# Out-projections of a two-layer diffusion backbone: residual and modulation steps by turns, z fetched in halves, read-back on GpSimd's queue, and a gMLP u phase in program order

## Chip, core and metric

The kernel runs on one core of one Trainium2 chip. The metric is the device time of one execution in microseconds (us). The engines are TensorE (PE in the profile; PEld is its weight load), VectorE (DVE), ScalarE (ACT), GpSimd (POOL) and SyncE (SP), which only issues transfers here.

## What is computed

512 latent tokens and 256 context tokens of width 1024 go through two layers. Each layer is FFN, mixer, FFN; the mixer is a gated MLP (gMLP) in layer 0 and grouped-query attention in layer 1. Every sub-layer is modulated by a shift, a scale and a gate, and closed by a LayerNorm. Everything is float32.

```python
def ffn_sublayer(x, shift, scale, gate, w_in, w_out, ln_g, ln_b):
    y = swiglu(x * (1 + scale) + shift, w_in, w_out)        # D_FF = 2816
    return layer_norm(ALPHA * x + 0.5 * gate * y, ln_g, ln_b)

def gmlp_mix(h, w_in, sgu_g, sgu_b, w_s, b_s, w_out):        # half width 3072
    u, v = split(gelu(h @ w_in), 2)
    v = layer_norm(v, sgu_g, sgu_b)
    v = einsum('gpq,bnqgc->bnpgc', w_s, v.reshape(...)) + b_s   # 8 groups, chunks of 128 tokens
    return (u * v) @ w_out

def modulation(cond, w_mod, b_mod):                          # 9 vectors of 1024 per layer
    return split(silu(cond) @ w_mod + b_mod, 9)              # for c and for c_ctx
```

The last sub-layers work on the latent tokens alone.

## The kernel before

**Numbers.** Each float32 operand is split into a high part and a remainder ("low"): ScalarE writes the high part, VectorE subtracts it. A product is three matmuls: high x high, high x low, low x high. The tokens lie in 6 blocks of 128 (4 latent, 2 context).

**Weights.** `load_raw` lets SyncE fetch raw weight tiles (256 KB, 6 buffers); `pump` turns them into split units `w` (8 buffers). `split_later` puts the low subtraction on a list, and `flush` issues the list.

**Order.** TensorE, SyncE and GpSimd's transfers issued through `self.pool` keep program order (`Pinned`). VectorE and ScalarE keep it only between `pin(True)` and `pin(False)`; elsewhere a scheduler may move their instructions. The u phase of gMLP runs unpinned.

**Fills.** The modulation vectors of later sub-layers are made in the background. `begin_sublayer` queues the units of `MOD_PLAN`; a unit is one of the nine vectors, for one or two conditions (`nconds`). Each call of `fill` does one of a unit's 16 steps: it takes a 256 KB tile of w_mod from `mraw`, does one VectorE step per condition into `acc`, and asks for the next tile. After eight steps GpSimd adds over the partitions (`partition_all_reduce`, L370) and sends the row away (L371). In an FFN's input projection `tile_strassen` calls it once per tile through `slot`, from f = 2 on. `End.begin` does what is left of the queue at one go.

**Activations.** The input projection makes 22 (FFN) or 24 (gMLP) tiles of 128 x 768. The last 4 stay in SBUF; the others are stored to DRAM by GpSimd (`act<-stage`). `Acts.feed` reads them back into `q` buffers (6 of them, two per tile, up to three tiles in hand) on SyncE's queue, and `prepare` splits a tile three tiles ahead of its use.

**Out-projection** (`out_proj`, for three FFNs and gMLP). Two halves of 512 columns; per half a loop over the tiles x: 18 matmuls each, a `pump`, a `prepare`, then VectorE work at the end of the tile. At x = 1 of half 0 the residual begins: all six blocks of z (512 KB each) and two rows of ln_g and ln_b are asked for on SyncE's queue, and from x = 3 on each tile multiplies and adds one half block (`residual`). Half 0 of z goes first, then a second pair of rows and half 1. Each of these tiles calls `fill` as well. In half 1 the result of half 0 is added to z in tiles 1 to 6 (`adds`). The last 6 tiles of half 1 are done block by block with the LayerNorm (`End`). The first FFN has no residual step (`prev` is None): z is the input. `out_proj_latent` is the same for the last FFN, with both halves at once.

**u phase of gMLP.** v was stored to DRAM before (`v_spill`). Each of 24 passes j does the spatial matmuls of v tile j, the projection of u tile j + 1, then on VectorE the six S steps that empty the spatial banks; v tile j + 1 is normalized (`normed`: ScalarE, then a split), the Gelu of u tile j is taken and multiplied by S. v tile j + 2 is fetched in pass j (`fetch`, three buffers); so a v tile is asked for one pass before it is normalized.

Of the kernel before, what the change touches and what calls it, by code (L numbers as in the profile page):

```python
# [63 lines left out]
    [(1, 5), (1, 2), (1, 3)],  # L64
    [(1, 6), (1, 4), (1, 7)],
    [],
# [19 lines left out]
class Backbone:  # L86
# [68 lines left out]
    def slot(self, post, n=1, fills=0):  # L155

        self.flush()
        self.pump(n)
        if self.combining is not None:
            post()  # L160
            if next(self.combining, self) is self:
                self.combining = None
        else:
            self.fill(fills)
            post()
# [182 lines left out]
    def mod_unit(self, l, i):  # L348

        nc, io = self.nc, self.io  # L350
        nconds = self.nconds(l, i)
        m = self.mods[l, i] = self.dram.tile([2, D], F32, name=f"mod{l}{i}")
        for c in range(nconds):
            self.pool.dma_start(m[c : c + 1, :], io["b_mod"][l, i * D : i * D + D].unsqueeze(0))
        for half in range(2):
            accs = [self.acc() for _ in range(nconds)]
            for k in range(KD):
                raw, dve = self.next_raw(), self.dve
                for c in range(nconds):
                    cs = self.cs[:, c * KD + k : c * KD + k + 1]  # L360
                    if k:
                        dve.scalar_tensor_tensor(accs[c], raw, cs, accs[c], ALU.mult, ALU.add)
                    else:
                        dve.tensor_scalar(accs[c], raw, cs, None, ALU.mult)
                self.filler_raw()
                if k < KD - 1:
                    yield
            s = slice(half * 512, half * 512 + 512)
            for c in range(nconds):
                nc.gpsimd.partition_all_reduce(accs[c], accs[c], P, bass_isa.ReduceOp.add)  # L370
                nc.gpsimd.dma_start(m[c : c + 1, s], accs[c][0:1, :], accum_op=ALU.add)  # L371
            yield
        self.mod_sent.add((l, i))
        if i % 3 == 2:
            self.mod_done.add((l, i))
        elif {(l, i - i % 3), (l, i - i % 3 + 1)} <= self.mod_sent:
            self.later(READ_LATER, lambda: self.mod_columns(l, i - i % 3))
# [22 lines left out]
    def residual(self, prev, nblocks):  # L400

        for b in range(nblocks):
            self.sp.dma_start(self.z[b], self.zsrc[b])
        if prev is None:
            return
        for half in range(2):
            s = slice(half * 512, half * 512 + 512)
            rows = []
            for name in ("ln_g", "ln_b"):
                row = self.zplace()  # L410
                src = self.io[name][prev[0], prev[1], s].unsqueeze(0)
                self.sp.dma_start(row, src.to_broadcast([P, 512]))
                rows.append(row)
            for _ in range(1 if half else 3):
                yield
            for b in range(nblocks):
                z = self.z[b][:, s]
                self.dve.tensor_tensor(z, z, rows[0], ALU.mult)
                self.dve.tensor_tensor(z, z, rows[1], ALU.add)
                yield  # L420

# [48 lines left out]
    def fill(self, n=1):  # L470

        for _ in range(n):
            with self.behind():
                for x in self.pending:
                    x[0] -= 1
                due = [x for x in self.pending if x[0] < 0]
                self.pending = [x for x in self.pending if x[0] >= 0]
                for _, f in due:
                    f()
                next(self.filler, None)  # L480

    @contextmanager
# [230 lines left out]
    def out_proj(self, acts, l, i, factor, end, prev, gate_at=2):  # L713
# [5 lines left out]
        self.new_z(NB)  # L719
        residual = iter(())  # L720
        st = self.stats(NB)
        banks, adds = {}, []
        for half, order in enumerate(orders):
            body = n - CLOSE * half
            for x in range(body):
# [15 lines left out]
                if not half and x == 1:  # L741
                    residual = self.residual(prev, NB)
                    next(residual, None)
                if not half and x == gate_at:
                    self.load_gate(l, i + 2, NB)
                if adds and x:
                    b, z, tmp = adds.pop(0)
                    self.dve.tensor_tensor(z, z, tmp, ALU.add)
                    self.dve.bn_stats(st[b][:, 0], z)
                else:  # L750
                    next(residual, None)
                if not half or x > 3:
                    acts.feed(half, 3 - half)
                if half or x < n - 2:
                    self.fill(1)
        for _ in residual:
            pass
        rest = [acts.of(f) for f in orders[1][n - CLOSE :]]
# [14 lines left out]
    def out_proj_latent(self, acts, l, i, factor, end, prev):  # L773
# [4 lines left out]
        self.new_z(NB_LAT)  # L778
        residual = iter(())
        banks = {}  # L780
        for x in range(n - CLOSE_LAT):
            ws = self.weights(2)
            for b in range(NB_LAT):
# [4 lines left out]
                if b % 2:  # L788
                    self.flush()
                    self.pump(1)  # L790
                    if b == 1:
                        acts.prepare(0, x + AHEAD + 1)
                        next(residual, None)
            self.release(2)
            acts.feed(0, 4)
            if x == 1:
                residual = self.residual(prev, NB_LAT)
                next(residual, None)
                self.load_gate(l, i + 2, NB_LAT)
        for _ in residual:  # L800
            pass
        st = self.stats(NB_LAT)
# [134 lines left out]
    def ffn(self, l, i, nblocks, end, prev):  # L937
# [4 lines left out]
        for f in range(FF):  # L942
            opened = self.begun.pop(min(self.begun)) if self.begun else None
            self.tile_strassen(lambda: acts.place(f), opened, int(f > 1))
            if not f:
# [120 lines left out]
    def gmlp(self, l, i, nblocks, end, prev):  # L1066
# [74 lines left out]

        fetch(0)
        fetch(1)
        var = self.const.tile([P, NB], F32, name="v_var")
# [29 lines left out]

        vns = [normed(3)]
        for j in range(GMLP_CH):
# [15 lines left out]
            banks = us.pop(0)  # L1192
            fetch(j + 2)
            m, done = acts.place(j)
# [6 lines left out]
            for step in range(2):  # L1201
                for bb in range(NB // 2):
# [4 lines left out]
                    )  # L1207
            if j + 1 < GMLP_CH:
                vns.append(normed(NB if j else 3))
            for x, ps in enumerate(banks):  # L1210
# [3 lines left out]
                dve.tensor_tensor(to, u[:, cols], S[:, cols], ALU.mult)  # L1214
                done(cols, to)
                self.flush()
            with nullcontext() if j else self.tc.issue_after(self.last_split):
                self.pump()
            self.fill(int(0 < j < GMLP_CH - 1))
# [435 lines left out]
    def body(self):  # L1655
# [4 lines left out]
        self.last_rstd = self.last_low = None  # L1660
        self.lows, self.slots, self.filler = [], False, iter(())
        self.setup()
# [19 lines left out]
class Acts:  # L1682
# [40 lines left out]
    def feed(self, half, most):  # L1723

        wanted = self.wanted[half]
        while len(self.raw) < most and wanted:
            f = wanted.pop(0)
            parts = []
            for o in range(0, self.ntok, self.width):
                raw = self.k.q(512)[:, 0 : self.width]  # L1730
                cols = slice(o, o + self.width)
                self.k.sp.dma_start(raw, self.dram[f][:, cols])
                parts.append((cols, raw))
# [160 lines left out]
```

## Time and profile before

| what | us |
|---|---|
| median of 3 runs (lowest, highest) | 2899.09 (2896.8, 2903.82) |
| profiled execution | 2898.31 |
| its span, first to last instruction | 2896.5 |
| busy: PE | 2795.1 |
| busy: DVE | 2108.4 |
| busy: ACT | 1163.6 |
| busy: POOL | 411.2 |

The profile is of one execution. A row of the timeline gives the start and the duration in us, the engine, the line of the kernel, the operation, what it writes <- what it reads, the shapes, how many instructions are merged, and in brackets how long the engine stood idle before and what ended that. Many operations go through a helper and carry its line, L81. SPq marks SyncE's issue of a transfer. A row of the stretches gives start:end and length, then for each engine its busy time and the number of instructions, the granted clock of TensorE, the busy share of the DMA engines and GB/s.

### The profile page before, as it was taken

The numbers are of one execution on the slowest core, as the hardware profiler recorded it, in microseconds if no ns is written. First come the engines' busy times: TensorE is split into PE (matmuls) and PEld (weight loads), VectorE is DVE, ScalarE is ACT, GpSimd is POOL, SyncE is SP. The second block draws the span as 40 slices with busy tenths as digits, with TensorE's granted clock in tenths as the row PEclk, the third lists the DMA queues.
The fourth block names the chain that finished last, engine by engine and source line by source line (L and its number), as shares of the span: only waits on it lengthen the run. The fifth ranks groups of instructions, "written<-read, shape, count | busy, mean of one in ns | idle before, by whom it ended". The sixth has DMA issues, their size and how long they took to land.

```text
span 2896.5 us, 40499 instructions
## 1 busy us (share of the span) xinstructions
PE 2795.1 (96%) x14454; PEld 2507.2 (87%) x14454; DVE 2108.4 (73%) x3692; ACT 1163.6 (40%) x2232; POOL 411.2 (14%) x379
## 2 busy tenths in 40 slices
PE   7899999999999999999999999999999989999998
PEld 5899988888899977889999788999978778888887
DVE  7988877577776787498787968877785578733445
ACT  6333432532344432453333226333432556633322
POOL 1010112234301112000010210000021121100001
PEclk9999999999999999999999999999999999999999
DMA  7433375355544474344335644433474423454352
GB/s 240 132 112 124 106 248 169 135 186 179 184 156 142 145 245 141 117 148 126 121 118 195 197 127 132 143 119 119 134 250 149 130 84 52 139 147 135 102 168 97
DMA packets 407090, 426.84 MB, mean 147 GB/s; under 512 B 27944, under 2 KB 308584, under 8 KB 406888
## 3 DMA queue, kind: packets, MB, share of 16 engines
q1 hardware_dynamic: 387400, 361.36, 40.3%
q0 software_dynamic: 19488, 62.90, 6.8%
q8 instruction: 113, 1.85, 0.3%
q14 instruction: 89, 0.73, 0.1%
HBM read 362.95 MB, written 63.41 MB: 147 GB/s over the span
## 4 chain that ended last, share of the span: by engine, by line
PE 72%; DVE 9%; DMA 8%; ACT 6%; issue 3%; SPq 1%; POOL 0%; DVEq 0%; ACTq 0%; POOLq 0%
PE ps L81 71%; DMA v<-v_spill 3%; ACT v L1135 2%; DVE w L81 2%; DVE acc L81 1%; DMA zraw<-in_ln_b_dram 1%; DVE w L148 1%; PE pp L81 1%; DMA q<-act 1%; SPq L81 1%; DVE z L81 1%; ACT w L147 1%; DMA mraw<-in_w_mod_dram 1%; ACT q L566 1%; DMA raw<-in_w_mod_dram 1%
## 5 line engine op out<-in xcount | busy, mean ns | idle before, releaser
L81 PE MATMUL ps<-comb,w 128*128 128x384 f32 x5544 | 974.1, 336 | 21.5 <-DVE comb L81 12.5
L81 PEld LDWEIGHTS ps<-comb,w 128*128 128x128 f32 x5544 | 963.9, 188 | 27.9 <-DVE comb L81 15.8
L81 PE MATMUL ps<-w,acts 128*128 128x512 f32 x3768 | 867.6, 391 | 19.6 <-DVE acts L81 19.3
L81 PEld LDWEIGHTS ps<-w,acts 128*128 128x128 f32 x3768 | 704.6, 188 | 174.7 <-DVE acts L81 29.1
L81 ACT CAST w<-raw 128x512 fp32r<-128x512 f32 x583 | 360.5, 619 | 732.3 <-PE ps L81 675.0
L81 DVE TENSOR_TENSOR w<-raw,w 128x512 fp32r<-128x512 f32 x583 | 426.8, 737 | 249.6 <-ACT w L81 249.5
L81 PE MATMUL ps<-h,w 128*128 128x384 f32 (+2 forms) x2304 | 447.9, 354 | 7.0 <-DVE su L1205 3.5
L81 PEld LDWEIGHTS ps<-h,w 128*128 128x128 f32 x2304 | 404.9, 189 | 45.1 <-DVE w L148 3.9
L370 POOL PARTITION_ALL_REDUCE acc<-acc x56 | 200.5, 3587 | 787.2 <-DVE acc L81 693.8
L81 PE MATMUL ps<-w,h 128*128 128x512 f32 x1200 | 278.5, 393 | 5.9 <-DVE kT L142 3.1
L81 PEld LDWEIGHTS ps<-w,h 128*128 128x128 f32 x1200 | 226.5, 190 | 54.9 <-ACT h L580 3.6
L81 DVE TENSOR_TENSOR q<-q,ps 128x384 f32<-128x384 f32 (+1 forms) x282 | 157.2, 558 | 151.0 <-PE ps L81 125.1
L81 DVE SCALAR_TENSOR_TENSOR acc<-mraw,cs,acc 128x512 f32<-128x512 f32 x340 | 248.3, 764 | 3.8 <-DMA mraw<-in_w_mod_dram 3.8
L81 ACT CAST w<-sums 128x512 fp32r<-128x512 f32 x198 | 122.9, 621 | 235.9 <-DVE sums L290 113.7
L81 ACT CAST acts<-q 128x384 fp32r<-128x384 f32 (+1 forms) x262 | 129.5, 521 | 199.4 <-DMA q<-act 160.2
L81 POOL DMA_DIRECT2D act<-stage x84 | 47.4, 565 | 995.3 <-DVE stage L81 803.2
L148 DVE TENSOR_TENSOR w<-raw,w 128x512 fp32r<-128x512 f32 x161 | 112.1, 714 | 77.3 <-ACT w L147 76.8
L81 DVE TENSOR_TENSOR acts<-q,acts 128x384 fp32r<-128x384 f32 (+1 forms) x262 | 138.5, 562 | 9.6 <-ACT acts L81 9.6
L81 DVE TENSOR_TENSOR w<-sums,w 128x512 fp32r<-128x512 f32 x198 | 135.6, 685 | 1.9 <-ACT w L81 1.9
L147 ACT CAST w<-raw 128x512 fp32r<-128x512 f32 x161 | 96.3, 619 | 57.1 <-PE ps L81 32.0
L174 POOL TENSOR_TENSOR rs<-ve,mhalf 128x1 f32<-128x1 f32 (+3 forms) x47 | 40.7, 867 | 491.5 <-DVE ve L171 260.9
L81 DVE TENSOR_TENSOR z<-z,zraw 128x512 f32<-128x512 f32 x88 | 72.9, 828 | 41.7 <-DMA zraw<-in_ln_g_dram 33.9
(193 smaller groups left out, 2122.0 us busy)
## 6 DMA issues: line engine op xcount, KB each, us to landing
raw<-in_ffn_w_in_dram SPq DMA_DIRECT2D x388, 256.0 KB
mraw<-in_w_mod_dram SPq DMA_DIRECT2D x256, 256.0 KB
raw<-in_ffn_w_out_dram SPq DMA_DIRECT2D x176, 256.0 KB
q<-act SPq DMA_DIRECT2D x216, 192.0 KB
act<-stage POOLq DMA_DIRECT2D x74, 384.0 KB, 2.7
raw<-in_gmlp_w_in_dram SPq DMA_DIRECT2D x96, 256.0 KB
zhat<-z POOLq DMA_DIRECT2D x26, 512.0 KB, 3.0
raw<-in_gmlp_w_out_dram SPq DMA_DIRECT2D x48, 256.0 KB
```

What stands on the lines that cost most here:

```text
L81: return self.tc.keep_in_program_order(f(*args, **kwargs))
L147: self.act.copy(hi, src)
L148: self.lows.append((key, lambda: self.dve.tensor_tensor(lo, src, hi.bitcast(F32), ALU.subtract)))
L174: self.last_rstd = self.nc.gpsimd.tensor_tensor(rs, ve, self.mhalf[:, 0:1].to_broadcast([P, n]), ALU.pow).ins
L370: nc.gpsimd.partition_all_reduce(accs[c], accs[c], P, bass_isa.ReduceOp.add)
L566: self.act.activation(h32[:, kk], ps[:, s], AF.Identity, bias=bi, scale=sc)
L1135: act.activation(vr[:, b], vr[:, b], AF.Identity, bias=n, scale=r)
```

## The change

- `residual` returns a list of steps. It loads one pair of rows and the first two half blocks of z; each step asks for the half block two steps on, and the last step of half 0 loads the second pair of rows. With no `prev` it loads z whole as before.
- In `out_proj` a residual step is done only in odd tiles of half 0 from x = 3 on, and in half 1 after the `adds`. A tile with a residual step or an `adds` step calls `fill` only where the unit in work is for one condition (`light`), or, beside `adds`, where there is no `prev`; the others call it once. `feed` moves ahead of these steps. In `out_proj_latent` the steps are done from x = 3 on.
- `slot` calls `fill_tile`: one fill, and a second one if the unit is `light`. Fills start at f = 1. In `MOD_PLAN` (1, 4) goes before (1, 6).
- The read-back goes to GpSimd's queue.
- u phase: three v tiles are fetched and two normalized ahead of the loop; in pass j, v tile j + 4 is fetched and j + 2 normalized, after the Gelu of u tile j. VectorE and ScalarE are pinned. `pump(2)` takes the place of `pump()`.

```diff
-    [(1, 6), (1, 4), (1, 7)],
+    [(1, 4), (1, 6), (1, 7)],
...
-            self.fill(fills)
+            if fills:
+                self.fill_tile()
...
                 raw, dve = self.next_raw(), self.dve
+                self.light = nconds == 1
...
+        def fetch(n):
+            if n < len(parts):
+                half, b = parts[n]
+                s = slice(half * 512, half * 512 + 512)
+                self.sp.dma_start(self.z[b][:, s], self.zsrc[b][:, s])
+
+        def step(n):
+            half, b = parts[n]
+            fetch(n + 2)
+            z = self.z[b][:, half * 512 : half * 512 + 512]
+            self.dve.tensor_tensor(z, z, rows[half][0], ALU.mult)
+            self.dve.tensor_tensor(z, z, rows[half][1], ALU.add)
+            if n == nblocks - 1:
+                load(1)
+
+        load(0)
+        fetch(0)
+        fetch(1)
+        return [lambda n=n: step(n) for n in range(len(parts))]
...
+    def fill_tile(self):
+
+        self.fill()
+        if self.light:
+            self.fill()
...
-                if adds and x:
-                    b, z, tmp = adds.pop(0)
-                    self.dve.tensor_tensor(z, z, tmp, ALU.add)
-                    self.dve.bn_stats(st[b][:, 0], z)
-                else:
-                    next(residual, None)
                 if not half or x > 3:
                     acts.feed(half, 3 - half)
-                if half or x < n - 2:
-                    self.fill(1)
+                if adds:
+                    if x:
+                        b, z, tmp = adds.pop(0)
+                        self.dve.tensor_tensor(z, z, tmp, ALU.add)
+                        self.dve.bn_stats(st[b][:, 0], z)
+                    self.fill(int(prev is None or self.light))
+                elif residual and x > 2 and (half or x % 2):
+                    residual.pop(0)()
+                    self.fill(int(self.light))
+                elif half or x < n - 1:
+                    self.fill()
...
-            self.tile_strassen(lambda: acts.place(f), opened, int(f > 1))
+            self.tile_strassen(lambda: acts.place(f), opened, int(f > 0))
...
-        vns = [normed(3)]
+        vns = [normed(3), normed(3)]
+        fetch(3)
+        self.pin(True)
+        dve, act = self.dve, self.act
...
-            fetch(j + 2)
+            fetch(j + 4)
...
-            if j + 1 < GMLP_CH:
-                vns.append(normed(NB if j else 3))
+            halves = []
             for x, ps in enumerate(banks):
                 cols = slice(x * HT, x * HT + HT)
                 act.activation(u[:, cols], ps, AF.Gelu)
                 to = (u if m is None else m)[:, cols]
                 dve.tensor_tensor(to, u[:, cols], S[:, cols], ALU.mult)
-                done(cols, to)
-                self.flush()
-            with nullcontext() if j else self.tc.issue_after(self.last_split):
-                self.pump()
+                halves.append((cols, to))
+            if j + 2 < GMLP_CH:
+                vns.append(normed())
+            for half in halves:
+                done(*half)
+            self.flush()
+            self.pump(2)
+            self.flush()
...
-                self.k.sp.dma_start(raw, self.dram[f][:, cols])
+                self.k.pool.dma_start(raw, self.dram[f][:, cols])
```

More of the change, by code (lines that the diff above doesn't have):

```diff
@@ L1 @@
-from contextlib import ExitStack, contextmanager, nullcontext
+from contextlib import ExitStack, contextmanager
 import concourse.bass as bass
@@ L400, in residual, with load @@
     def residual(self, prev, nblocks):
-        for b in range(nblocks):
-            self.sp.dma_start(self.z[b], self.zsrc[b])
         if prev is None:
[L405 to L408, printed above, removed]
+            for b in range(nblocks):
+                self.sp.dma_start(self.z[b], self.zsrc[b])
+            return []
+        rows = {}
+        parts = [(half, b) for half in range(2) for b in range(nblocks)]
+        def load(half):
+            rows[half] = []
             for name in ("ln_g", "ln_b"):
                 row = self.zplace()
-                src = self.io[name][prev[0], prev[1], s].unsqueeze(0)
+                src = self.io[name][prev[0], prev[1], half * 512 : half * 512 + 512].unsqueeze(0)
                 self.sp.dma_start(row, src.to_broadcast([P, 512]))
[L413 to L420, printed above, removed]
+                rows[half].append(row)
+        def fetch(n):
[15 more added lines that the diff above has]
+        return [lambda n=n: step(n) for n in range(len(parts))]
     def residual_begin(self, prev, nblocks):
@@ L719, in out_proj @@
         self.new_z(NB)
-        residual = iter(())
+        residual = []
         st = self.stats(NB)
@@ L742, in out_proj @@
                     residual = self.residual(prev, NB)
-                    next(residual, None)
                 if not half and x == gate_at:
                     self.load_gate(l, i + 2, NB)
-                if adds and x:
-                    b, z, tmp = adds.pop(0)
-                    self.dve.tensor_tensor(z, z, tmp, ALU.add)
-                    self.dve.bn_stats(st[b][:, 0], z)
-                else:
-                    next(residual, None)
                 if not half or x > 3:
                     acts.feed(half, 3 - half)
-                if half or x < n - 2:
-                    self.fill(1)
-        for _ in residual:
-            pass
+                if adds:
[9 more added lines that the diff above has]
+                    self.fill()
+        assert not residual
         rest = [acts.of(f) for f in orders[1][n - CLOSE :]]
@@ L778, in out_proj_latent @@
         self.new_z(NB_LAT)
-        residual = iter(())
+        residual = []
         banks = {}
@@ L792, in out_proj_latent @@
                         acts.prepare(0, x + AHEAD + 1)
-                        next(residual, None)
+                        if residual and x > 2:
+                            residual.pop(0)()
             self.release(2)
@@ L797, in out_proj_latent @@
                 residual = self.residual(prev, NB_LAT)
-                next(residual, None)
                 self.load_gate(l, i + 2, NB_LAT)
-        for _ in residual:
-            pass
+        assert not residual
         st = self.stats(NB_LAT)
@@ L1140, in normed @@
             return m
-        fetch(0)
-        fetch(1)
+        for j in range(3):
+            fetch(j)
         var = self.const.tile([P, NB], F32, name="v_var")
@@ L1660, in body @@
         self.last_rstd = self.last_low = None
-        self.lows, self.slots, self.filler = [], False, iter(())
+        self.lows, self.slots, self.filler, self.light = [], False, iter(()), False
         self.setup()
```

## The prediction

> **What bounds the kernel now.** I read the page from the top first: the span, the busy shares and the chain.
>
> ```profile
> span 2896.5 us, 40499 instructions
> PE 2795.1 (96%) x14454; PEld 2507.2 (87%) x14454; DVE 2108.4 (73%) x3692; ACT 1163.6 (40%) x2232; POOL 411.2 (14%) x379
> PE 72%; DVE 9%; DMA 8%; ACT 6%; issue 3%; SPq 1%; POOL 0%; DVEq 0%; ACTq 0%; POOLq 0%
> ```
>
> TensorE is the bound, and 28% of the chain is not matmul. The change adds and removes no matmul, so it can win only time in which TensorE waits. The second view, stretches chosen by stage, shows where that is.
>
> ```profile
> core 0: us, PE busy (x) PEld busy (x) DVE busy (x) ACT busy (x) POOL busy (x), PEclk, DMA share, GB/s
> 2550.00:2850.00 300.00, 300.00 (x1326) 248.47 (x1325) 121.95 (x185) 89.28 (x150) 13.29 (x13) 1.00 0.47 141
> 125.00:375.00 250.00, 250.00 (x1442) 249.39 (x1441) 213.49 (x357) 96.73 (x176) 26.39 (x25) 1.00 0.38 116
> 1300.00:1550.00 250.00, 250.00 (x1444) 250.00 (x1443) 202.56 (x342) 95.80 (x173) 18.13 (x22) 1.00 0.38 119
> 791.00:1021.00 230.00, 223.25 (x1330) 220.48 (x1331) 164.54 (x335) 109.86 (x243) 29.93 (x32) 0.98 0.47 147
> 1021.78:1203.00 181.22, 173.73 (x756) 140.56 (x755) 126.26 (x201) 53.94 (x107) 28.57 (x14) 1.00 0.57 183
> 1562.49:1727.00 164.51, 157.39 (x687) 127.86 (x687) 127.36 (x193) 47.93 (x94) 36.05 (x18) 1.00 0.62 199
> 2085.84:2250.00 164.16, 159.12 (x688) 129.28 (x688) 113.82 (x182) 48.31 (x94) 25.81 (x13) 0.99 0.62 199
> ```
>
> The first row is the clean rate of a 512-column matmul: 300.00/1326 = 0.2262 us, so an out-projection tile of 18 takes 4.07. The next two are input projections with TensorE never idle. The fourth is the gMLP u phase, the last three the out-projections of gMLP, FFN (0,6) and FFN (1,0). By the count they lose 181.22 - 756 x 0.2262 = 10.2 us, 164.51 - 687 x 0.2262 = 9.1 and 164.16 - 688 x 0.2262 = 8.5: 27.8 in all. The third view, the timeline of the gMLP out-projection, says why.
>
> ```profile
> 1030.53 3.89 SPq L81 DMA_DIRECT2D z<-zhat  x6
> 1036.58 1.59 SPq L81 DMA_DIRECT2D q<-act  x2
> 1043.54 0.69 DVE L81 TENSOR_TENSOR z<-z,zraw 128x512 f32<-128x512 f32 x1 [6.66 <-DMA zraw<-in_ln_g_dram]
> 1046.49 1.05 ACT L81 CAST acts<-q 128x384 fp32r<-128x384 f32 x2 [7.19 <-DMA q<-act]
> 1047.55 3.66 POOL L370 PARTITION_ALL_REDUCE acc<-acc  x1 [55.80 <-DVE acc L81]
> 1048.02 2.73 DVE L81 TENSOR_TENSOR w<-raw,w 128x512 fp32r<-128x512 f32 x1
> 1055.84 0.80 POOL L371 DMA_DIRECT2D mod<-acc  x1 [0.30 <-POOL acc L370]
> 1057.33 25.21 PE L81 MATMUL ps<-w,acts 128*128 128x512 f32 x108 [1.68 <-DVE acts L81]
> 1058.99 1.41 DVE L81 SCALAR_TENSOR_TENSOR acc<-mraw,cs,acc 128x512 f32<-128x512 f32 x2
> 1060.32 0.68 DVE L81 TENSOR_TENSOR w<-raw,w 128x512 fp32r<-128x512 f32 x1
> 1060.92 1.02 DVE L81 TENSOR_TENSOR acts<-q,acts 128x384 fp32r<-128x384 f32 x2
> 1061.86 1.41 DVE L81 TENSOR_TENSOR z<-z,zraw 128x512 f32<-128x512 f32 x2
> 1063.18 1.41 DVE L81 SCALAR_TENSOR_TENSOR acc<-mraw,cs,acc 128x512 f32<-128x512 f32 x2
> 1080.40 0.69 DVE L81 TENSOR_TENSOR z<-z,zraw 128x512 f32<-128x512 f32 x1 [3.02 <-DMA zraw<-in_ln_g_dram]
> 1084.52 4.38 PE L81 MATMUL ps<-w,acts 128*128 128x512 f32 x18 [1.99 <-DVE acts L81]
> ```
>
> Six whole blocks of z (3 MB) are asked for at once; the ln rows and the next read-backs queue behind them. VectorE, in program order here, stands 6.66 us before the first residual step, the read-back cast 7.19. VectorE then cannot catch up: each tile holds a residual step, a modulation step and two splits, 1.41 + 1.41 + 0.68 + 1.02, read off the starts as 4.19 us (1058.99 to the same step at 1063.18), against TensorE's 4.07. Each reduction on GpSimd stretches a split from 0.68 to 2.73 and costs about 2 us more, and the second pair of rows waits another 3.02. So TensorE is left waiting for acts (1.68, 1.99).
>
> The u phase has another cause.
>
> ```profile
> 870.48 6.88 POOL L370 PARTITION_ALL_REDUCE acc<-acc  x2 [0.19 <-DVE acc L362]
> 874.14 3.04 DVE L142 TENSOR_TENSOR vn<-v,vn 128x768 fp32r<-128x768 f32 x1 [0.45 <-ACT vn L141]
> 879.25 0.43 SPq L81 DMA_DIRECT2D v<-v_spill  x1
> 885.58 0.88 ACT L1135 ACTIVATE v<-v,v_nb,rs 128x128 f32<-128x128 f32 x2 [9.20 <-DMA v<-v_spill]
> 892.84 2.71 PE L81 MATMUL ps<-w_sT,vn 128*128 128x256 f32 x11 [2.09 <-DVE vn L142]
> 870.10 1.59 PE L81 MATMUL ps<-w_sT,vn 128*128 128x256 f32 x12
> 879.88 1.67 PE L81 MATMUL ps<-w_sT,vn 128*128 128x256 f32 x12
> ACT v L1135 <- DMA v<-v_spill: 85.0, 20, 9.2
> 791.04 9.89 PE L81 MATMUL ps<-h,w 128*128 128x384 f32 x48 [2.91 <-DVE su L1205]
> ```
>
> A clean pass takes 879.88 - 870.10 = 9.78 us for 60 matmuls, so 1330 cost 216.8 of the 230: 13.2 us lost. The v tile is fetched one pass ahead, behind weight loads on SyncE that wait for VectorE; after a reduction pair it lands late, ScalarE stands before it 20 times (85.0 us from 800 to 1022), and now and then the spatial matmuls stand too. The last row is the wait at the phase's start.
>
> **The change part by part.**
>
> *Residual and modulation by turns.* Odd tiles from x = 3 do a residual step, even ones a modulation step: 1.41 + 0.68 + 1.02 = 3.11 us on VectorE, 0.96 below TensorE's 4.07, so it catches up by a tile's wait in about four. Twelve residual steps then reach into half 1. Modulation steps (fills) must still fit, because what is left at the end runs in one lump. Counted from the code: gMLP 54 + 22 + 13 + 10 = 99 for 96; FFN (0,6) 29 + 12 + 7 = 48 for 48; FFN (1,0) 26 + 22 = 48 for 48. Nothing is left. In FFN (1,0) the units are for one condition and share a tile with the residual step:
>
> ```profile
> 2161.44 0.74 DVE L81 SCALAR_TENSOR_TENSOR acc<-mraw,cs,acc 128x512 f32<-128x512 f32 x1
> ```
>
> 1.41 + 0.74 + 0.68 + 1.02 = 3.85, still under 4.07, and only in every other tile.
>
> *z in halves.* At x = 1 SyncE now issues two rows and two halves (1 MB) in place of 3 MB and two rows, then one half per step, two steps (four tiles, 16 us) ahead; the first use is two tiles (8 us) later. A modulation tile moves 256 + 256 + 384 KB, a residual tile as much (z half for w_mod), 896 KB per 4.07 us: about 225 GB/s, all the time and without the burst; the page's slices of 72 us (the row below) reach 250. The second pair of rows is asked two tiles before its use, not one: 4 us more for a wait of 3.02. The latent out-projection gets the same halves and later steps; it lies in the first clean row, so 0.
>
> *Read-back on GpSimd's queue.* 226 transfers leave SyncE's queue, where they stood with weights, w_mod and z behind them, for GpSimd's, where only the reductions with their sends, the activation stores and the z stores stand. GpSimd now waits for the q buffer, and the reductions behind that wait are wanted only some fills later. The nearest row is its own store of the same tensor:
>
> ```profile
> L81 SPq DMA_DIRECT2D q<-act x226: 319/376/1049, 384.6 to 2839.1; - x113
> L81 POOL DMA_DIRECT2D act<-stage x84: 539/542/893, 98.2 to 2638.2; - x84
> DMA to landing us min/median/max: 2.6/2.7/5.7
> GB/s 240 132 112 124 106 248 169 135 186 179 184 156 142 145 245 141 117 148 126 121 118 195 197 127 132 143 119 119 134 250 149 130 84 52 139 147 135 102 168 97
> ```
>
> Two per tile are 1.08 us (at most 1.79) of 4.07, and 2.7 to 5.7 to landing. A read is asked at a tile's end and cast 2.5 tiles (10.2 us) later; acts are split three tiles (12.2 us) before use. A reduction pair with its sends holds the queue from 1047.55 to 1056.64, 9.1 us, so after a pair a cast may be 9.1 + 1.1 + 2.7 - 10.2 = 2.7 us late, at worst 5.7; the three tiles cover it. I take 0, with a loss of 4 per pair (the middle) as the far end. Below nothing it cannot go by itself; what SyncE gains is in the burst's term.
> [...]
>
> So of 27.8 us I expect 1.5 per out-projection to stay (one late tile, as 1.68 to 1.99 above): **-23.3**. Ends: -26 (nearly all goes) and -12 (a wait of about 2 after each of two or three reductions stays, 5.3 per stage).
>
> *u phase.* v is fetched three tiles at the start and then four ahead (two passes before its normalization) and normalized two ahead, so a fetch 9.2 us late is covered by a pass of 9.78. The Gelu comes before the normalization on ScalarE, so a bank no longer waits behind a v that has not landed. The price is program order on VectorE and ScalarE. VectorE has 164.54 of 230 us there, 72%, so 7.0 of a pass's 9.78; a reduction pair may add the 2 x 2.1 us of the split above, 11.2, and the pass after it takes that back. Banks are reused a pass later, so TensorE need not see it. Of 13.2 lost I let 3 stay: **-10**. Ends: -13 (all) and -4 (only the waits for v's transfer as in the row of 2.09, twice). At the start two normalizations now precede everything, where the wait was 2.91 for the first S tiles; these no longer stand behind stretched weight splits: **-1**, between -3 and +2 (a normalization of about 2 us more ahead of S).
>
> *Fills in the input projections.* FFN (0,6) does 29 for 20, nine more of two conditions: 9 x 1.41 = 12.7 us over the stage, 10.5 of each 250: 202.6 to 213 us, just what 125 to 375 shows with TensorE at 250.00. FFN (1,0) does 26 for 20, 16 of them of two conditions for 4: 12 x 1.41 - 6 x 0.74 = 12.5. Free by that row; were the cover gone, 12.7 and 12.5. I take **+1** for a pair of reductions in an unlucky place, ends 0 and +2. The first FFN (58 fills for 56) and the order of w_mod units: 0.
>
> *Sum.* -23.3 - 10 - 1 + 1 = -33.3. The profiled execution took 2898.31 us (span 2896.5 and 1.8 around it): 2865.0. The median, 2899.09, is 0.8 above it: **2866 us**. With the ends: -26 - 13 - 3 + 0 = -42 gives 2857; -12 - 4 + 2 + 2 = -12 gives 2887.
>
> **The rivals.** (A) *Read-backs late behind the reductions.* GpSimd's queue takes the place of SyncE's: with 4 us lost per pair, uncovered, three pairs in gMLP and three in FFN (0,6), 24 us of the 23.3 come back; the u phase and the start stay: 2899 - 10 = 2889. For it: the 9.1 us hold. Against: three tiles of acts in hand.
> (B) *u phase unchanged*, because in program order VectorE itself is late after a pair (6.88 us of reductions, 3.04 for one split): 2899.1 - 23.3 + 1 = 2877. Against: 72% busy.
> (C) *The out-projections keep their waits* since the transfers, not their order, are late: DMA share 0.57 to 0.62 over those stages speaks against it, an average though. Only the u phase gains: 2889.
> (D) *Slower: GpSimd's issue becomes the pace.* If VectorE's operations stretch an issue as a reduction stretches theirs (2.73/0.68 = 4.0, so 0.542 becomes 2.17 us), two take 4.34 per tile, 0.27 over TensorE, on 30 + 3 x 26 = 108 read-back tiles: +29, and the out-projections' gain is gone: 2899 - 10 + 29 = 2918. It decides from 2.03 us per issue on. Against: 893 ns at most.
>
> **How the numbers follow.** Forecast 0.64, A 0.12, B 0.10, C 0.08, D 0.06. The runs shown lie within 0.24%, so 0.3% (8.7 us, 2890.4) is about what a measurement can tell. The forecast and B lie below it; A and C at 2889 are faster by 0.35%, so half of each counts as the same. Faster 0.64 + 0.10 + 0.10 = 0.84, same 0.10, slower 0.06. The range runs from 2854 (a little under the best ends, since all four places lose 27.8 + 13.2 + 2.91) to 2888, which leaves out most of A and C, and D.
>
> **What would show it.** In the profile after: matmul counts in 50 us of the out-projections near 221; VectorE's wait before z under 2 us in place of 6.66; TensorE's waits for acts under 2 us in each out-projection; q<-act issued on POOL at about 0.55 us each; ScalarE's 85.0 us for v gone; the u phase near 220 us. The forecast is wrong if POOL's issues exceed 2 us, if TensorE waits for acts right after each reduction pair, or if input projections show TensorE idle.

## The result and the profile after

The changed kernel takes 2878.76 us (median of four runs, 2876.56 to 2881.59); the kernel before, run beside it on the same chip, 2897.95. The ratio is 0.9931, 95% interval 0.9919 to 0.9943: faster by 0.7%, where 1.1% was forecast. The profiled execution lost 19.9 us of span for the 33.3 of the sum. The top of the page after, its span, shares, chain, the matmuls of the out-projections and the moved issues:

```profile
span 2876.6 us, 40697 instructions
PE 2790.9 (97%) x14454; PEld 2513.6 (87%) x14454; DVE 2098.9 (73%) x3692; ACT 1160.1 (40%) x2232; POOL 533.2 (19%) x605
PE 86%; DVE 6%; ACT 3%; issue 2%; DMA 2%; POOL 1%; SPq 0%; DVEq 0%; POOLq 0%; ACTq 0%
L81 PE MATMUL ps<-w,acts 128*128 128x512 f32 x3768 | 860.8, 390 | 0.0
L81 POOL DMA_DIRECT2D q<-act x226 | 127.1, 595 | 556.8 <-DVE acts L81 317.5
```

The 3768 matmuls of all out-projections now wait for nothing (fourth row; the last figure is the idle time before them). On the page of the kernel before, the same row has 19.6 us:

```profile
L81 PE MATMUL ps<-w,acts 128*128 128x512 f32 x3768 | 867.6, 391 | 19.6 <-DVE acts L81 19.3
```

The chain is 86% matmul in place of 72. The shares do not say why only 20 us came of it; a table by stage does. Each stage runs from its first matmul to the first of the next, worked out from the two traces (us):

| stage | before | after | difference |
|---|---|---|---|
| start, with the first input projection | 381.45 | 382.13 | +0.7 |
| out-projection (0,0) and gMLP v phase | 385.26 | 385.69 | +0.4 |
| gMLP u phase | 254.84 | 236.58 | -18.3 |
| gMLP out-projection | 210.57 | 200.19 | -10.4 |
| FFN (0,6) input projection | 330.37 | 338.93 | **+8.6** |
| FFN (0,6) out-projection | 192.97 | 193.65 | **+0.7** |
| FFN (1,0) input projection | 330.38 | 334.48 | **+4.1** |
| FFN (1,0) out-projection | 193.89 | 185.57 | -8.3 |
| attention, with the latent input projection | 486.17 | 489.00 | +2.8 |
| latent out-projection | 130.64 | 130.40 | -0.2 |

Stretches of the changed kernel, in the columns of the second view of the prediction: the u phase, the three out-projections (the second without its last tiles), and 250 us of the FFN (0,6) input projection.

```profile
core 0: us, PE busy (x) PEld busy (x) DVE busy (x) ACT busy (x) POOL busy (x), PEclk, DMA share, GB/s
784.00:1004.00 220.00, 220.00 (x1360) 219.33 (x1359) 175.02 (x352) 117.87 (x258) 41.55 (x40) 1.00 0.54 164
1004.40:1185.60 181.20, 180.45 (x801) 149.21 (x800) 127.09 (x204) 54.38 (x108) 59.11 (x70) 1.00 0.54 177
1543.52:1700.00 156.48, 156.48 (x692) 129.54 (x692) 109.83 (x176) 47.28 (x94) 48.10 (x61) 1.00 0.60 191
2071.66:2235.46 163.80, 163.80 (x722) 135.00 (x721) 101.56 (x171) 47.70 (x95) 40.29 (x58) 1.00 0.58 189
1255.00:1505.00 250.00, 245.02 (x1396) 243.82 (x1395) 213.90 (x360) 90.38 (x164) 27.44 (x27) 0.99 0.43 133
```

The first four are clean: 692 x 0.2262 = 156.5 of 156.48 us, 722 x 0.2262 = 163.3 of 163.80. The last is the place the sum did not hold: 1396 matmuls in 250 us, 48 fewer than the same length held before. The turns themselves can be read in the timeline of the gMLP out-projection:

```profile
1022.17 1.42 DVE L81 TENSOR_TENSOR z<-z,zraw 128x512 f32<-128x512 f32 x2 [2.98 <-DMA z<-zhat]
1029.81 30.54 PE L81 MATMUL ps<-w,acts 128*128 128x512 f32 x134
1031.77 3.68 DVE L81 TENSOR_TENSOR acts<-q,acts 128x384 fp32r<-128x384 f32 x2
1036.86 2.48 POOL L81 DMA_DIRECT2D q<-act  x4
1041.18 0.56 DVE L81 TENSOR_TENSOR acts<-q,acts 128x384 fp32r<-128x384 f32 x1 [1.02 <-ACT acts L81]
1043.51 0.56 DVE L81 TENSOR_TENSOR acts<-q,acts 128x384 fp32r<-128x384 f32 x1 [1.77 <-ACT acts L81]
1046.85 1.41 DVE L81 TENSOR_TENSOR z<-z,zraw 128x512 f32<-128x512 f32 x2
1049.72 1.41 DVE L81 SCALAR_TENSOR_TENSOR acc<-mraw,cs,acc 128x512 f32<-128x512 f32 x2
1052.59 1.41 DVE L81 TENSOR_TENSOR z<-z,zraw 128x512 f32<-128x512 f32 x2
1055.79 1.41 DVE L81 SCALAR_TENSOR_TENSOR acc<-mraw,cs,acc 128x512 f32<-128x512 f32 x2
```

z, acc, z, acc, one a tile. VectorE goes through a tile in 2.87 us there (1046.85 to 1049.72 to 1052.59), so it catches up by 1.2 us a tile. The reductions still stretch a pair of splits (3.68 against 1.02) and still hold GpSimd's queue, so that four read-backs go out in a lump at 1036.86 and the next splits are 1.02 and 1.77 late; TensorE runs through all of it.

The two new losses, first the one in FFN (0,6)'s second activation tile, then the one at the end of its out-projection (timeline):

```profile
1239.93 13.52 SPq L81 DMA_DIRECT2D raw<-in_ffn_w_in_dram  x6
1253.50 1.46 SPq L81 DMA_DIRECT2D mraw<-in_w_mod_dram  x3
1256.64 0.48 DVE L81 TENSOR_SCALAR acc<-mraw,cs 128x512 f32<-128x512 f32 x1
1259.14 0.75 DVE L81 SCALAR_TENSOR_TENSOR acc<-mraw,cs,acc 128x512 f32<-128x512 f32 x1 [2.02 <-DMA mraw<-in_w_mod_dram]
1259.81 0.55 DVE L81 TENSOR_TENSOR q<-pieces,ps 128x384 f32<-128x384 f32 x1
1260.41 31.77 PE L81 MATMUL ps<-comb,w 128*128 128x384 f32 x168 [3.99 <-DVE q L81]
...
1696.83 3.66 POOL L372 PARTITION_ALL_REDUCE acc<-acc  x1 [15.23 <-DVE acc L81]
1701.39 3.44 POOL L372 PARTITION_ALL_REDUCE acc<-acc  x1
1705.13 0.79 POOL L373 DMA_DIRECT2D mod<-acc  x1 [0.30 <-POOL acc L372]
1705.39 0.15 DVE L172 TENSOR_SCALAR ve<-mv 128x1 f32<-128x1 f32 x1
1713.09 0.59 POOL L175 TENSOR_TENSOR rs<-ve,mhalf 128x1 f32<-128x1 f32 x1 [7.17 <-issue]
1715.20 1.97 PE L81 MATMUL ps<-ident,z 128*128 128x128 f32 x8 [8.28 <-ACT z L1841]
```

Upper half: SyncE asks for the w_mod tile of the new modulation steps only at 1253.50, after six weight loads that it began at 1239.93. VectorE stands 2.02 us before it, program order holds the q step that frees the bank, and TensorE stands 3.99. Its granted clock is half for 6.83 us from 1258.7. Lower half: the last modulation step sets off the last pair of reductions, which ends at 1704.83. `rs`, the small power operation by which the first normalization begins, has its input at 1705.54 and starts at 1713.09 with nothing on GpSimd in between but the rest of the send (to 1705.92) and two configuration records (MODIFY_POOL_CONFIG, at 1705.74 and 1705.78). TensorE stands 8.28 us, and the clock is half for 10.24 from 1709.2. Before, the same records fell into a pause of 31 us and the wait was 0.75:

```profile
1733.60 0.60 POOL L174 TENSOR_TENSOR rs<-ve,mhalf 128x1 f32<-128x1 f32 x1 [31.39 <-DVE ve L171]
1735.72 1.09 PE L81 MATMUL ps<-ident,z 128*128 128x128 f32 x8 [0.75 <-ACT z L1811]
```

### The profile page after: what moved, and what is told of

It is laid out like the page before. It is cut to its first block, busy times and chain, and to the rows that moved or that the text cites. A ratio compares the mean times of both kernels' runs of the same rounds, so it can differ in the third digit from the quotient of the medians.

```text
span 2876.6 us, 40697 instructions
## 1 busy us (share of the span) xinstructions
PE 2790.9 (97%) x14454; PEld 2513.6 (87%) x14454; DVE 2098.9 (73%) x3692; ACT 1160.1 (40%) x2232; POOL 533.2 (19%) x605
## 4 chain that ended last, share of the span: by engine, by line
PE 86%; DVE 6%; ACT 3%; issue 2%; DMA 2%; POOL 1%; SPq 0%; DVEq 0%; POOLq 0%; ACTq 0%
PE ps L81 85%; PE pp L81 1%; DVE w L81 1%; ACT q L590 1%; DVE comb L81 1%; DVE z L81 1%; ACT z L1841 1%; DMA raw<-in_w_mod_dram 1%; DMA raw<-in_ffn_w_in_dram 1%; POOL acc L372 0%; POOL rs L175 0%; DVE q L81 0%; DVE w L148 0%; ACT h L590 0%; DMA mraw<-in_w_mod_dram 0%
## 5 line engine op out<-in xcount | busy, mean ns | idle before, releaser
L81 DVE TENSOR_TENSOR w<-raw,w 128x512 fp32r<-128x512 f32 x631 | 456.3, 731 | 293.4 <-ACT w L81 293.4
L81 DVE SCALAR_TENSOR_TENSOR acc<-mraw,cs,acc 128x512 f32<-128x512 f32 x378 | 275.2, 763 | 6.7 <-DMA mraw<-in_w_mod_dram 6.5
L81 POOL DMA_DIRECT2D q<-act x226 | 127.1, 595 | 556.8 <-DVE acts L81 317.5
L148 DVE TENSOR_TENSOR w<-raw,w 128x512 fp32r<-128x512 f32 x113 | 74.7, 687 | 29.0 <-ACT w L147 28.6
```

The costliest lines, as they stand in the source:

```text
L81: return self.tc.keep_in_program_order(f(*args, **kwargs))
L148: self.lows.append((key, lambda: self.dve.tensor_tensor(lo, src, hi.bitcast(F32), ALU.subtract)))
```

## The experiments

All are edits of the changed kernel. e1 and e2 were run four times, the others once: 2879.59 us (e3), 2864.73 (e4), 2885.98 (e5), 2887.38 (e6), 2879.69 (e7), 2878.64 (e8), 2887.91 (e9), 2881.85 (e10), 2884.04 (e11) and 2896.11 (e12). These runs differ by several us in the start (380.4 to 385.6 us) and in the attention stage (484.8 to 495.7, last section); no edit touches the attention, and of the start only its fills are touched, in e2, e4 and e12. So each verdict is read from the stage that the edit touches.

**What ate the gain?** e1 does a fill in the `adds` tiles of half 1 as well (gMLP's too), so that FFN (0,6) is done with its 48 steps earlier and no reduction stands right before `rs`, where TensorE waits 8.28 us.

```
-                    self.fill(int(prev is None or self.light))
+                    self.fill()
```

> The changed kernel, except that the tiles of half 1 which add half 0 to z do a modulation step as well, so FFN (0,6) is done with its 48 steps nine tiles before the end of its loop instead of in the last tile. [...] Then that wait falls to the 0.75 us of the kernel before, and the span falls by 9 to 10 us from 2876.6 to about 2867. Rival: the wait belongs to something else at the stage's end (a late z half block, say); then the span stays at 2876.

Measured: the stage came to 184.31 us from 193.65, the wait before the first normalization to 0.75 us. The time is 2871.55 us, ratio to the kernel before 0.9887 (0.9870 to 0.9903). The span fell only 1.4 us, since the attention took 495.51 with its clock at half for 23.9 us, against 13.7 in the changed kernel.

e2 adds to that the old bound of the input projections' fills, so that the second activation tile has none.

```
-            self.tile_strassen(lambda: acts.place(f), opened, int(f > 0))
+            self.tile_strassen(lambda: acts.place(f), opened, int(f > 1))
```

> As the kernel before it in this list, and the modulation steps of the FFN input projections start at f = 2 again, as in the kernel before the change. Theory: the 8.6 us that the input projection of FFN (0,6) and the 4.1 us that the one of FFN (1,0) gained come from the steps at f = 1, which VectorE meets while it is still behind after the opening and whose w_mod tiles SyncE asks for only after tile 0. Then both stages return to 330.4 us and the span is about 2854 to 2856. Rival: the doubled steps of the later tiles load VectorE and the transfers; then the stages stay at 336 and 333 or so, and the span at about 2862 to 2867.

Measured: **2860.99 us, ratio 0.9857 (0.9842 to 0.9872)**, better than both kernels. The input projections are back at 330.87 and 330.34 us (before: 330.37 and 330.38), so the whole +8.6 and +4.1 came from that one tile. The timeline of e2, the same tile and the same first normalization:

```profile
1249.72 15.59 PE L81 MATMUL ps<-comb,w 128*128 128x384 f32 x89
1254.24 1.45 SPq L81 DMA_DIRECT2D mraw<-in_w_mod_dram  x3
1684.81 14.44 PE L81 MATMUL ps<-w,acts 128*128 128x512 f32 x63
1697.88 0.60 POOL L175 TENSOR_TENSOR rs<-ve,mhalf 128x1 f32<-128x1 f32 x1 [19.91 <-DVE ve L172]
1700.00 1.10 PE L81 MATMUL ps<-ident,z 128*128 128x128 f32 x8 [0.75 <-ACT z L1841]
```

The w_mod tiles are asked for at the same place, but nobody waits for them yet. No reduction stands before `rs`, which is there in time.

e3 lets only one more of the last tiles do a fill (`or x == 6`), so that the last reductions come earlier by less. If the pause before `rs` (7.17 us) only follows the pair, a tile of 4.1 us earlier leaves 8.28 - 4.1 = 4.2 us of TensorE's wait at the first normalization.

> The changed kernel with one modulation step more in half 1 (tile 6), so the last pair of reductions of FFN (0,6) starts one tile, 4.1 us, earlier. [...] Rival (the pair itself was late; it ended at 1705.92 and the power operation was wanted at 1705.54): 0.4 us earlier would have been enough, and the wait falls to about 0.75.

Measured: the stage 189.71 us, TensorE's wait 5.01:

```profile
1702.04 3.44 POOL L372 PARTITION_ALL_REDUCE acc<-acc  x1
1705.78 0.79 POOL L373 DMA_DIRECT2D mod<-acc  x1 [0.30 <-POOL acc L372]
1713.63 0.59 POOL L175 TENSOR_TENSOR rs<-ve,mhalf 128x1 f32<-128x1 f32 x1 [7.06 <-issue]
1715.74 1.97 PE L81 MATMUL ps<-ident,z 128*128 128x128 f32 x8 [5.01 <-ACT z L1841]
```

GpSimd's pause is the same 7 us (configuration records at 1706.39 and 1706.43, `rs` 7.24 after the first; 7.35 in the changed kernel). The wait shrank only because the reductions ended earlier against the need: 3.15 us earlier from the stage's start, where a tile of 4.1 was expected, so 5.01 was left in place of about 4.2. So the price is that pause, when a power operation is wanted right behind a reduction; the two runs show it at this one place.

e4 is e1 with one fill in place of two in the second activation tile when the units are of one condition (main line of its edit; `f` is handed down to it).

```
-        if self.light:
+        if self.light and f > 1:
```

> As the first kernel of this list, but at f = 1 only one modulation step is done where the changed kernel does two. Theory: of the 3.99 us that TensorE waited at f = 1 in FFN (0,6), 2.02 + 0.75 are the second step, whose w_mod tile had not landed; the input projection of FFN (0,6) comes to 332 to 334 us in place of 338.9, and that of FFN (1,0), where the one step at f = 1 is of two conditions, stays at 334.5. Rival: one step at f = 1 is as bad as two, since the SyncE queue is what falls behind; then 338 to 339 us stay.

Measured: 332.59 us for FFN (0,6)'s input projection, the wait in that tile 1.62 us; FFN (1,0), where the tile's unit is one of two conditions either way, unchanged at 334.67. The second fill's w_mod tile was the larger part; one fill is still too early.

**What won in the out-projections?** e5 puts the read-backs back on SyncE's queue (`self.k.sp.dma_start(raw, ...)`), e6 asks for all twelve halves of z at x = 1, with `fetch(n + 2)` gone, e10 does both, e7 undoes the turns alone, and e11 all three. e12 is e11 with the order of w_mod units and the fills of the input projections as before, too.

```
-                elif residual and x > 2 and (half or x % 2):
+                elif residual and x > 2:
                     residual.pop(0)()
-                    self.fill(int(self.light))
+                    self.fill()
```

(the edit of e7)

```
-    [(1, 4), (1, 6), (1, 7)],
+    [(1, 6), (1, 4), (1, 7)],
...
         self.fill()
-        if self.light:
-            self.fill()
...
-            self.tile_strassen(lambda: acts.place(f), opened, int(f > 0))
+            self.tile_strassen(lambda: acts.place(f), opened, int(f > 1))
```

(what e12 adds to e11)

> The changed kernel with the read-back on SyncE's queue as before; z in halves and the turns stay. Theory: the read-back was late only because 3 MB of z stood ahead of it, so with halves it is early enough on either queue: gMLP's out-projection (start of its first matmul to the next stage's) stays at 200 to 201 us (210.6 before, 200.2 after), FFN (1,0)'s at 185.5 to 186.5 (193.9, 185.6). Rival: the move of the queue carries part of the gain; then 203 or more, and 188 or more.

> The changed kernel with all twelve half blocks of z asked for at tile 1, ahead of the ln rows (3 MB at once, as before); the turns and the read-back on GpSimd's queue stay. Theory: VectorE again stands some 6 us before its first residual step, but with the turns it has about 1 us per tile to catch up and TensorE has three tiles of acts in hand: gMLP's out-projection 200 to 202 us, FFN (1,0)'s 185.5 to 187. Rival: the burst itself costs TensorE 2 us or more per stage; then 202.5 and 188 or more.

> The changed kernel without the turns: a residual step and a modulation step in every tile from x = 3 on until the twelve residual steps are done. z in halves and the read-back on GpSimd's queue stay. Theory: VectorE needs 4.19 us per tile against 4.07, and a reduction pair adds 4 us that it cannot win back, so TensorE waits once the three tiles in hand are used up: gMLP's out-projection 203 to 207 us. In FFN (1,0), with steps of one condition (3.5 us per tile), at most 187. Rival: the burst was the whole cause; then 200 to 201.

> The changed kernel with both transfer edits undone together: all twelve halves of z asked for at once at x = 1, and the read-backs on SyncE's queue; only the turns of residual and modulation steps are left in the out-projections. Theory: the turns carry the gain, so the gMLP out-projection stays at 200 to 202 us (200.2 with the whole change, 210.6 before) and that of FFN (1,0) at 185.5 to 186.5 (193.9 before). Rival: the two transfer edits stand in for each other, which is why undoing each alone cost nothing; then undoing both brings 3 us or more back, gMLP 203 to 207 us, with a first wait of VectorE for z or its rows of over 4 us.

> As the run before, and the turns undone as well (a residual step and a fill in each tile from x = 3, all of z asked for at once, read-backs on SyncE's queue); the u phase and the rest stay as in the changed kernel. Theory: the gMLP out-projection is back at 208 to 212 us, so that the turns are worth 8 to 10 us with the transfers as before and 5.5 with the new ones (205.7 without turns), and half of the loss before was the late transfers that the turns make harmless. Rival: the loss before hung on the generator's late start (residual steps from x = 1), and without it the transfers matter little: 205 to 207 us.

| out-projection, us | before | after | e5 read-back on SyncE | e6 burst | e10 both, turns only | e7 no turns | e11 none |
|---|---|---|---|---|---|---|---|
| gMLP | 210.57 | 200.19 | 200.60 | 200.83 | 200.43 | 205.67 | 212.11 |
| FFN (0,6) | 192.97 | 193.65 | 193.11 | 193.07 | 193.33 | 186.19 | 189.32 |
| FFN (1,0) | 193.89 | 185.57 | 185.55 | 185.57 | 185.59 | 185.59 | 185.98 |

The turns alone (e10) bring the gMLP stage to 200.43: the whole gain. All these runs do the same 40 modulation steps on VectorE and the same 6 reductions in that stage as the kernel before. e10's rival, that the transfer edits stand in for each other, falls: VectorE stood 7.1 us before its first residual step in e10, and 10.9 in e6 where some 6 were expected, and TensorE did not wait. e11's rival, the later start of the residual steps, falls too. Without turns the transfers do matter: 205.67 with the new ones, 212.11 with the old. What TensorE waited for in that stage (the waits of e11, then of e7; us in total, times, longest):

```profile
PE ps L81 <- DVE acts L81: 8.7, 5, 2.4
```

```profile
PE ps L81 <- DVE acts L81: 3.8, 3, 1.9
```

These are the waits of before (1.68, 1.99) again; the same view of e10 holds no row of acts at all. FFN (0,6) is shorter without turns because its last step then comes earlier and `rs` does not wait. So in the changed kernel as it stands the turns win 5.5 us in gMLP (e7) and lose 7.5 in FFN (0,6); they pay in both only with e1's fills.

FFN (1,0) is at 185.6 to 186.0 in all of them, e11 too, so neither the turns nor the transfers won 8.3 us there. The trace offers another cause: the units of two conditions are now done in the input projection. With them the stage lost 18 of its 40 modulation steps on VectorE (about 0.74 us each), and 3 of its 6 reductions on GpSimd, since theirs come in pairs; e11 has the lower counts too. e12 brings these units back.

> As the kernel with all three edits undone (gMLP out-projection 212.11 us, FFN (1,0) 185.98), and in addition the order of the w_mod units of FFN (1,0) and the fills of the input projections are those of before (one fill a tile, from the third activation tile on), so that two-condition units with pairs of reductions fall into FFN (1,0)'s out-projection again: 6 reductions there before, 3 in the changed kernel. Theory: those pairs were the loss, so this stage is back at 191 to 195 us (193.89 before), with 5 or 6 reductions in it. Rival: the later start of the residual steps (x = 3 in place of 1) won those 8 us; then it stays at 185.5 to 187.5 us whatever the units are. In both cases the two FFN input projections return to 330 to 331 us (338.9 and 334.5 in the changed kernel).

Measured: 194.05 us, and 330.38 and 330.74 for the two input projections. The reductions in FFN (1,0)'s out-projection in the kernel before, in e11 and in e12 (shortest, median and longest in ns, first and last start), with e12's wait of TensorE:

```profile
L370 POOL PARTITION_ALL_REDUCE acc<-acc x6: 3232/3524/3660, 2110.8 to 2216.2; - x6
```

```profile
L372 POOL PARTITION_ALL_REDUCE acc<-acc x3: 3230/3599/3599, 2108.6 to 2168.3; - x3
```

```profile
L372 POOL PARTITION_ALL_REDUCE acc<-acc x6: 3229/3466/3659, 2100.0 to 2201.8; - x6
PE ps L81 <- DVE acts L81: 5.2, 4, 2.2
```

So that stage gained by the units of two conditions that left it. The expectation put it down to their pairs of reductions alone; that is not shown, because e12 brings back the steps as well. The longest wait of e12 comes before its second pair, which starts at 2139.80, and behind the late second pair of rows, while VectorE takes its 4.19 us a tile and cannot catch up (timeline of e12):

```profile
2128.30 0.69 DVE L81 TENSOR_TENSOR z<-z,zraw 128x512 f32<-128x512 f32 x1 [1.38 <-DMA zraw<-in_ln_g_dram]
2133.10 9.17 PE L81 MATMUL ps<-w,acts 128*128 128x512 f32 x32 [2.22 <-DVE acts L81]
```

Of what moved these units, the fills at f = 1 cost the two input projections their 12.7 us and are not needed for the gain: without them, in e2, FFN (1,0)'s out-projection takes 186.39. In FFN (0,6), with 8 reductions before and in e12 and 6 in e11, the units are worth part: 195.21 in e12, 189.32 in e11.

**What won in the u phase?** e8 keeps the new order of the phase (Gelu first, program order) with v fetched and normalized one pass ahead as before. e9 keeps the old order and fetches v three tiles ahead, normalized one ahead.

```
e8: -        vns = [normed(3), normed(3)]      e9: -            fetch(j + 4)
    +        vns = [normed(3)]                     +            fetch(j + 3)
    -            fetch(j + 4)                      (and the loop's order of before)
    +            fetch(j + 2)
```

> The changed kernel with v fetched and normalized one pass ahead as before; program order and the Gelu ahead of the normalization stay. Theory: the u phase's waits came from v landing late, so with program order alone the phase stays long: 246 us or more (254.8 before, 236.6 after), only the wait at its start goes. Rival: what counted was that Gelu, S steps and weight splits no longer stand behind v and behind each other; then 237 to 240.

> The changed kernel with the u phase as before (planned order, the Gelu behind the normalization of v, v normalized one pass ahead), except that v is fetched three tiles at the start and then three ahead. Read at the stage from the first u matmul to the first of the gMLP out-projection: 254.8 us before, 236.6 with the whole change, 241.5 with the order alone. If the order carries the gain (my theory after the run with the order alone), the stage stays at 247 to 254 us. If the late fetch of v was the cause and either cure would do (the rival, and what the prediction said), it comes to 238 to 243 us. ScalarE's wait for v's transfer (85.0 us before) should fall under 25 us in both cases.

Measured: 241.47 us for e8, between its theory and its rival, and 243.31 for e9; it was 254.84 before and 236.58 with both. After e8 I took the order for the cause and the late fetch for a bystander; e9 refutes that, and I had expected ScalarE's wait under 25 us there, which came to 55.7. Either cure alone takes 11.5 to 13.4 of the 18.3 us. ScalarE in e9, 785 to 1010 us, then TensorE's waits there, e9 and e8 (us in total, times, longest):

```profile
ACT v L1159 <- DMA v<-v_spill: 55.7, 20, 7.2
PE ps L81 <- DVE su L1229: 3.3, 1, 3.3
PE ps L81 <- ACT su L1236: 1.2, 1, 1.2
```

```profile
PE ps L81 <- DVE vn L81: 3.3, 1, 3.3
```

ScalarE still stands 20 times before v in e9, but at most 7.2 us in place of 9.2, and TensorE never stands inside the phase. What is left in both are waits at its start (786.63 and 790.64 us in e9, 787.86 in e8), with half clock for 6.83 and 3.41 us. In the changed kernel, where two tiles of v are normalized before the phase, neither wait is there.

## Why the prediction was right, and where its sum was not

The direction held and the time lies in the range, 13 us above the forecast. That it came so near is partly luck, as the steps show: the gains were 11.4 us larger than booked (27.4 + 18.3, with e1's fills, against 34.3), two losses took 22.0 us where 1 was booked, and stages that the sum put at 0 or left out added 3.7. Of the prediction's own signs of being wrong, one appeared: TensorE idle in an input projection (3.99 us). Step by step:

- **"Nothing is left"** is the step that failed first. The count (48 steps for 48) was right, but I read it as a comfort. With nothing to spare, the last step falls into the last tile, and its reductions stand on GpSimd right before the power operation of the first normalization. The sum had no term for that; it cost 193.65 - 184.31 = 9.3 us (e1).
- **"Fills in the input projections", +1, ends 0 and +2**, measured 8.6 + 4.1 = 12.7 us. "Free by that row" took a mean over 250 us for a property of each tile. VectorE did have the room (213.90 of 250 us, 213 forecast); what the row cannot show is that the second tile's w_mod load queues on SyncE behind six weight loads. This step named no queue.
- **Residual and modulation by turns**, -23.3: measured -10.4 and -8.3, and 192.97 - 184.31 = -8.7 in FFN (0,6) with e1's fills; -27.4 together. In gMLP the mechanism was right (e10) and only the size too small: the late tile of 1.5 us that I let stay did not stay. In FFN (1,0) the gain came, but by another part of the change: the units of two conditions that moved into the input projection (e12). In FFN (0,6) the turns are the smaller part too: 195.21 us in e12, 189.32 with those units moved (e11), 186.19 with the new transfers (e7), 184.31 with the turns and e1's fills. The sum booked the move of the units as a cost of +1 and nothing else, though it had the lighter steps (3.85 us a tile) and had named the pairs of reductions as what stretches the splits.
- **z in halves** cost and won nothing beside the turns in gMLP and FFN (1,0) (e6). VectorE's first wait was 2.98 us, not under 2, and harmless.
- **Read-back on GpSimd's queue**, 0: right, and unneeded (e5). The 226 issues took 595 ns on average, 1022 the longest, with VectorE busy 109.83 of 156.48 us in an FFN out-projection.
- **u phase**, -10 and -1, measured -18.3. I let 3 us stay inside the phase and none did. At the start I gave 1 us where the two waits (2.91 and 1.38 before) and the half clock beside them (3.41 us) went altogether.

With e1 and e2's repairs the profiled span is 2859.2 us, 37.3 under before, though its attention is 5.7 us longer: the sum of -33.3 was near, with too little in the gains and no term for the two losses.

Rivals: **A** was there in kind (the lump of read-backs at 1036.86, splits late by 1.02 and 1.77 us) and the acts in hand covered it, as argued. **B** named 2877, close to what came, but by luck: its mechanism did not occur, and the u phase gained most of all. **C** falls by e10, in which the transfers are those of before and TensorE does not wait. **D** falls by the 595 ns; it needed 2.03 us.

## What to carry to other kernels

A stage's busy share shows that an engine has room on average. Before filling that room, look at the first tile that gets the new work, and at which queue its data stands in. When a list of background steps just fits, ask what the last one triggers and who needs that engine next; slots to spare were worth 9 us here. And two cures for one lateness may each do most of the work alone, so undo them one at a time and together before saying which one did it.

## What the hardware showed that I had not expected

**GpSimd paused for 7 us between a reduction and a power operation.** From the configuration record to the start of `rs` it took 7.35 and 7.24 us (changed kernel, e3) with the input ready; the rows above have 7.17 and 7.06 us of idle before it. None shows what GpSimd does in the pause.

**Two short idles of TensorE cost more than themselves.** The granted clock went to one half in pieces of 3.41 us, up to three at the waits read here. At the waits of 3.99 and 8.28 us it was half for 6.83 and 10.24 us; of this, 5.07 and 4.25 us lie behind the wait's end (1260.41 and 1715.20). In those 5.07 us TensorE began 16 matmuls, in the 5.07 behind them 31; its first 8 behind the second wait took 1.97 us, the same 8 at full clock 1.04 (from 1722.25). So by estimate half of those stretches, some 2.5 and 2.1 us, was lost on top of the waits. The attention stage shows it, with the same matmuls in e8 and then e1:

```profile
2262.00:2746.75 484.75, 465.54 (x2446) 398.13 (x2445) 283.56 (x576) 222.87 (x432) 56.70 (x63) 1.00 0.42 118
```

```profile
2249.31:2744.82 495.51, 473.68 (x2446) 404.78 (x2444) 284.37 (x575) 223.62 (x431) 56.88 (x63) 0.98 0.41 115
```

Half clock held for 3.41 us in the first and 23.9 in the second. In the kernel before it was 6.83 (486.17 us), in the changed kernel 13.66 (489.00); but e12 took 494.47 with 13.66, so it is not the only thing that varies there. Behind which of the short idles the clock drops, and why, was not tried. The stage's spread of 11 us over the kernels, which all compute it alike, is as large as most of the gains here, so the last microseconds of a comparison are best read by stage.
